# Attention queries stored per head over all 128 partitions, with the other head's rows zero

## The chip, the core and the metric

The kernel runs on one core of a Trainium2 chip. The metric is the device time of one execution in microseconds (us). Besides TensorE (PE, with its weight loads listed apart as PEld), the core has VectorE (DVE), ScalarE (ACT), GpSimd (POOL) and SyncE (SP), each with its own instruction queue.

## The reference, cut to what matters

One decoder layer over 512 tokens of 2048 channels: an RMS norm, one wide input projection, four token mixers (a gated linear recurrence, pooling, a short convolution, an attention), four gates, an output projection, and an MLP. The change is in the attention alone: 8 heads of 64 channels, queries and keys normalised per head, swept in 4 blocks of 128 queries.

```python
q = rms_norm(q.reshape(b, s, 8, 64), q_g)
k = rms_norm(k.reshape(b, s, 8, 64), k_g)
logits = einsum('bqhd,bkhd->bhqk', qi, k) * 64 ** -0.5
logits = logits + (cqi[..., :, None] - cum[..., None, :])
p = softmax(where(key_pos <= q_pos, logits, -inf))
out = einsum('bhqk,bkhd->bqhd', p, v)
```

## The kernel before, in words

Activations lie transposed: channels on the 128 partitions, the 512 tokens along a row. Two neighbouring heads therefore share one tile: the even head lies on partitions 0 to 63, the odd head on 64 to 127. There are four such pairs.

Every large product runs in fp32 accuracy as three products (`mm3`, line 182): each operand is split into a high part rounded to fp32r and a low part, the rest (`split`, line 213: ACT writes the high part, line 218, or line 221 with a per-partition scale; DVE writes the low part, line 219, or line 222 with the scale). The first operand of `mm3` is the stationary one (it is loaded as weights), the second streams through.

Weights come in chunks of 1024 columns by DMA on SP's queue, are split by ACT (line 150) and DVE (line 151), and are held in three buffers, so that two chunks are ready while one is used (`chunk`, line 155).

For each pair `i`, `pair` (line 487) projects queries and keys and hands them to `qk_norm` (line 350), which computes the per-head norm and at its end, line 363, calls `split` into tiles of the tag "m" (16 buffers of 128x512). Four tiles of "m" hold the values throughout. Then `attend` (line 427) does for each of 4 query blocks `t` and both heads `b` what `probabilities` (line 439) says: one `mm3` of a 128-token query block (stationary) against the keys up to it (streaming 256, 256, 384 or 512 columns) into a bank `pl`, the forget bias (DVE, line 446), the causal mask (POOL, line 450), the softmax (DVE and ACT, lines 455 to 458). It takes the head's half of the tiles, `r = slice(64 * b, 64 * b + 64)`, so these products use 64 of the 128 rows of the array. Next come the transposes of the probabilities (`pt`, line 179), their copy (`pT`, ACT, line 475) and the product with the values (`po`, line 480), whose output takes 64 of the 128 columns of the array.

The order on PE is that of the program text. The attention steps are generators that are resumed from within the projections: `poll` (line 203), called after each `mm3` of a projection, resumes a step when a counter of estimated PE time has passed its due time. The counter uses the number of columns of a product, not its rows. So each attention step stands alone between projection products (`pgb`, `pq`, `pk`, `pb` and so on, 128 rows by 512 columns). The order on ACT and DVE up to line 1121 is chosen at build time by the framework's scheduler; from there on it is that of the text.

After the attention (it ends near 530 us) follow the gates, the output projection and the MLP in a Strassen-like form with products of 128x256, from about 640 us to the end.

Of the kernel before, what the change touches and what calls it, by code (L numbers as in the profile page):

```python
# [15 lines left out]
P = 128  # L16
# [82 lines left out]
def body(nc, tc, ctx, dram):  # L99
# [3 lines left out]
    V, A, G, T = nc.vector, nc.scalar, nc.gpsimd, nc.tensor  # L103

    def const(name, shape, dt=F32):
        return pool.tile(shape, dt, name=name, tag=f"c_{name}", bufs=1)
# [18 lines left out]
    def t512(tag, name, dt=F32, rows=P):  # L125
        return stage[tag].tile([rows, S], dt, name=name, tag=tag, bufs=BUFS[tag])

    def bank(name, tag="mm"):
        return psum.tile([P, 512], F32, name=name, tag=tag, bufs=4)

    def f(x):
        return x.bitcast(F32)
# [39 lines left out]
    def mm(out, w, x, start, stop, more=False):  # L172
        T.matmul(out, w, x, start=start, stop=stop, skip_group_check=more)  # L173
        n = x.shape[-1]
        clock[0] += (max(n, 2 * P) if x.dtype == F32R else 4 * max(n, P)) / 2400

    def tr(out, x):
        n = x.shape[0]
        T.transpose(out, x, ident[:n, :n])
        clock[0] += P / 1200  # L180

    def mm3(out, w, x, first=True, last=True, more=False):

        n = x[0].shape[-1]
        mm(out[:, :n], w[0], x[0], first, False, more)
        mm(out[:, :n], w[0], x[1], False, False, more)
        mm(out[:, :n], w[1], x[0], False, last, more)
# [25 lines left out]
    def split(src, tag, name, scale=None):  # L213

        hi = t512(tag, f"{name}h", F32R)
        lo = t512(tag, f"{name}l", F32R)
        if scale is None:
            A.copy(hi, src)
            V.tensor_tensor(out=lo, in0=src, in1=f(hi), op=ALU.subtract)
        else:  # L220
            A.mul(hi, src, scale)
            V.scalar_tensor_tensor(out=lo, in0=src, scalar=scale, in1=f(hi), op0=ALU.mult, op1=ALU.subtract)
        return hi, lo
# [15 lines left out]
    def pc(name, i=0, rows=P):  # L239
        c = _COLS[name][0] + i  # L240
        return par[:rows, c : c + 1]
# [7 lines left out]
    for k in range(KT):  # L249
        h, r = divmod(k, 8)  # L250
# [37 lines left out]
    def inv_sqrt(y, ms, v, s):  # L288

        A.activation(s, ms, AF.Sqrt)  # L290
        recip(y, s)
        V.tensor_tensor(out=v, in0=ms, in1=y, op=ALU.mult)
        V.tensor_tensor(out=v, in0=v, in1=y, op=ALU.mult)
        V.tensor_scalar(v, v, -0.5, 1.5, ALU.mult, ALU.add)
        V.tensor_tensor(out=y, in0=y, in1=v, op=ALU.mult)
# [45 lines left out]
    def proj(c, name, given=None, tag="y"):  # L341
# [2 lines left out]
        V.tensor_tensor(out=o, in0=ps, in1=n1[1], op=ALU.mult)  # L344
        return o

    qg8 = const("qg8", [P, 1])
    V.tensor_scalar(qg8, pc("qg"), 0.125, None, ALU.mult)

    def qk_norm(src, g, name):  # L350
        sq = t512("y", f"{name}sq")
        A.activation(sq, src, AF.Square)
        hi, lo = split(sq, "y", f"{name}q")
        yield 10
        ms = bank(f"{name}ms", "aux")
        mm(ms, eblk, hi, True, False)
        mm(ms, eblk, lo, False, True)
        v, s = t512("y", f"{name}v"), t512("y", f"{name}s")
        V.tensor_scalar(v, ms, EPS, None, ALU.add)
        inv_sqrt(sq, v, v, s)  # L360
        V.scalar_tensor_tensor(out=src, in0=src, scalar=g, in1=sq, op0=ALU.mult, op1=ALU.mult)
        yield 5
        qk[name] = split(src, "m", f"{name}n")

    def log1p_exp_neg_abs(z, mk, name):

# [28 lines left out]
    qk = {}  # L395
# [31 lines left out]
    def attend(i):  # L427
        qn, kn = qk[f"q{i}"], qk[f"k{i}"]
        y = t512("k", f"yd{i}")
        ys[3].append(y)  # L430
        ncb = []
        for b in range(2):
            h = 2 * i + b
            n = t512("g", f"ncb{h}")
            nc.sync.dma_start(n, ncd[h : h + 1].to_broadcast([P, S]))
            ncb.append(n)
        yield 4

        def probabilities(t, b):
            h = 2 * i + b  # L440
            r = slice(64 * b, 64 * b + 64)
            span = (t + 1) * P
            pl = bank(f"pl{h}{t}", "aux")
            mm3(pl, [p[r, t * P : span] for p in qn], [p[r, : max(span, 2 * P)] for p in kn])
            l = t512("y", f"l{h}{t}")
            V.scalar_tensor_tensor(
                out=l[:, :span], in0=ncb[b][:, :span], scalar=cumT[:, t * 8 + h : t * 8 + h + 1],
                in1=pl[:, :span], op0=ALU.add, op1=ALU.add,
            )
            G.affine_select(  # L450
                out=l[:, t * P : span], in_=l[:, t * P : span], compare_op=ALU.is_ge, fill=NEG,
                base=0, pattern=[[-1, P]], channel_multiplier=1,
            )
            st = pool.tile([P, 4], F32, name=f"st{h}{t}", tag="st", bufs=6)
            V.tensor_reduce(st[:, 0:1], l[:, :span], axis=AX.X, op=ALU.max, negate=True)
            A.activation(l[:, :span], l[:, :span], AF.Exp, bias=st[:, 0:1], accum_out=st[:, 1:2])
            V.reciprocal(st[:, 2:3], st[:, 1:2])
            V.tensor_scalar(l[:, :span], l[:, :span], st[:, 2:3], None, ALU.mult)
            return l

        steps = [(t, b) for t in range(TT) for b in range(2)]
        ahead = [probabilities(*steps[0])]
        yield 4
        ahead.append(probabilities(*steps[1]))
        for n, (t, b) in enumerate(steps):
            h = 2 * i + b
            yield 4
            l = ahead.pop(0)
            if n + 2 < len(steps):
                ahead.append(probabilities(*steps[n + 2]))  # L470
            pt = bank(f"pt{h}{t}", "aux")
            for k in range(t + 1):
                tr(pt[:, k * P : (k + 1) * P], l[:, k * P : (k + 1) * P])
            pT = t512("y", f"pT{h}{t}")
            A.copy(pT[:, : (t + 1) * P], pt[:, : (t + 1) * P])
            yield 4
            if b == 0:
                po = bank(f"po{i}{t}", "aux")
            for k in range(t + 1):
                mm(  # L480
                    po[64 * b : 64 * b + 64, :P], val[k][:, h * 64 : (h + 1) * 64],
                    pT[:, k * P : (k + 1) * P], k == 0, k == t,
                )
            if b == 1:
                A.copy(y[:, t * P : (t + 1) * P], po[:, :P])

    def pair(i):
        q = proj(XQ + i * P, f"q{i}")
        chain(qk_norm(q, qg8, f"q{i}"))
        k = proj(XK + i * P, f"k{i}")  # L490

        def steps():
            yield from qk_norm(k, pc("kg"), f"k{i}")
            yield 12
            yield from attend(i)

        chain(steps())
# [7 lines left out]
    for t in range(TT):  # L505
        V.tensor_scalar(zt[:, t * 8 : (t + 1) * 8], vb[t][:, nv:VW], n1[0][:, t : t + 1], None, ALU.mult)
        A.mul(val[t][:, W - nv :], vb[t][:, :nv], n1[0][:, t : t + 1])
    chain(forget(zt))
    chain(qk_norm(first[0], qg8, "q0"))


# [308 lines left out]
    def result(name, where, tag, cols):  # L820

        for t in list(later):
            if t[3] < era[0]:
                pop(t)
        era[0] += 1
        return wide(name, where, tag, 2, cols)
# [107 lines left out]
    def wide(name, where, tag, bufs, cols=7 * H):  # L934
        return where[1].tile([P, cols], F32, name=name, tag=tag, bufs=bufs)

    def half_wide(name, where):
        return wide(name, where, "u", 1, S)
# [122 lines left out]
    for k in range(4):  # L1061
# [24 lines left out]
        if k == 3:  # L1086
            yk = y3

            p, ip = t512("p", "p"), t512("p", "ip")
# [8 lines left out]
        else:  # L1098
            yk, y3 = y2, [split(y, "s", f"y3{q}") for q, y in enumerate(ys[3])]
            for j in (6, 7, 0, 1, 2, 3, 4, 5):  # L1100
                x = wide(f"x_{j}", lz[0], "z", 2, 1024)
                t = wide(f"xs{j}", st1, "st1", 1)
# [10 lines left out]
        for j in range(8):  # L1113
            for e, ps in rows(f"branch{k}", 0, j, yk, f"pb{k}"):
                n = 2 * j + e
                t = t512("g", f"b{k}{n}")
# [105 lines left out]
    for e in range(2):  # L1222
        hi, lo = (t512("q", f"mg{q}{7 + 8 * e}", F32R) for q in "hl")
        src = merged[0][:, e * S : (e + 1) * S]
# [178 lines left out]
    for n, phase in enumerate(down_pairs, 2):  # L1403
        r, u = result(f"y{n}", dpool, "r", 1024), half_wide(f"ud{n}", dpool)
# [97 lines left out]
```

## Time and profile before

| | us |
|---|---|
| median of 3 runs | 2746.12 (2743.14 to 2746.85) |
| the profiled execution's own time | 2745.49 |
| span of its trace | 2743.7 |
| PE busy | 2711.5 (99% of the span) |
| PEld busy | 2544.5 (93%) |
| DVE busy | 2137.7 (78%) |
| ACT busy | 1223.0 (45%) |
| POOL busy | 156.5 (6%) |

The profile is of one execution of the 2745.49 us. A busy PE is not a PE at its peak: a product is recorded from its start to a modelled end, which overlaps the next one. What a product costs in a stream is the distance from its start to the next start; the timeline shows it. Mean granted clock of PE: 0.997 of full speed.

### The profile page before, as it was taken

Reading aid. Unit: us, or ns where it says so; the run is one execution under the profiler, and the core shown is the slowest. Engines: PE = TensorE matmul, PEld = TensorE weight load, DVE = VectorE, ACT = ScalarE, POOL = GpSimd, SP = SyncE. Lnnn points to the kernel's source line nnn. Section 1 sums busy time; section 2 is a strip of 40 time slices with the busy share of each in tenths; the row PEclk is TensorE's granted clock in tenths of the full one; section 3 lists DMA queues with packets and bytes.
Section 4 is the critical chain, followed back from the end, with each engine's and each line's share of the span. In section 5 each row is a group of like instructions: output and inputs, shape, how many; then the busy total and the mean of one; then the engine's idle time right before and its main releaser. Section 6 shows DMA issues by size and latency. Waiting matters only on the chain. (4 is left out here: it accounts for less than half of the span.)

```text
span 2743.7 us, 48190 instructions
## 1 busy us (share of the span) xinstructions
PE 2711.5 (99%) x19952; PEld 2544.5 (93%) x19952; DVE 2137.7 (78%) x2641; ACT 1223.0 (45%) x1506; POOL 156.5 (6%) x283
## 2 busy tenths in 40 slices
PE   8999999999999999999999999999998999999999
PEld 7787777789999999998888999999998999999999
DVE  6865664386888888887549988888887788888887
ACT  5443344454444444443324444444444444444443
POOL 0000000000000000003010000000000000000000
PEclk9999999999999999999999999999999999999999
DMA  5222223474444444447453544444446656666575
GB/s 198 86 93 85 81 81 125 163 231 159 145 154 147 152 133 155 143 142 256 144 176 123 173 164 145 163 148 161 149 141 228 183 177 182 182 174 190 169 217 145
DMA packets 143900, 429.48 MB, mean 157 GB/s; under 512 B 16696, under 2 KB 30904, under 8 KB 143680
## 3 DMA queue, kind: packets, MB, share of 16 engines
q1 hardware_dynamic: 101536, 279.19, 29.9%
q0 software_dynamic: 32496, 129.65, 16.2%
q10 hardware_dynamic: 9648, 17.57, 1.7%
q8 instruction: 156, 2.56, 0.4%
q14 instruction: 64, 0.52, 0.1%
HBM read 350.04 MB, written 79.97 MB: 157 GB/s over the span
## 5 line engine op out<-in xcount | busy, mean ns | idle before, releaser
L731 ACT CAST uhd<-wqd 128x1024 fp32r<-128x1024 f32 (+2 forms) x128 | 130.8, 1024 | 230.3 <-PE pdd L173 86.8
L731 ACT CAST uhg<-wqg 128x1024 fp32r<-128x1024 f32 (+1 forms) x136 | 135.5, 999 | 184.8 <-PE pgd L173 94.3
L731 ACT CAST uhu<-wqu 128x1024 fp32r<-128x1024 f32 (+1 forms) x144 | 136.2, 952 | 160.1 <-PE pud L173 85.2
L741 DVE TENSOR_TENSOR uld<-wqd,uhd 128x1024 fp32r<-128x1024 f32 (+2 forms) x128 | 151.8, 1187 | 69.6 <-ACT uhd L731 69.6
L151 DVE TENSOR_TENSOR wl<-wr,wh 128x1024 fp32r<-128x1024 f32 (+2 forms) x100 | 117.4, 1175 | 91.1 <-ACT wh L150 90.8
L741 DVE TENSOR_TENSOR ulg<-wqg,uhg 128x1024 fp32r<-128x1024 f32 (+1 forms) x136 | 157.1, 1157 | 31.7 <-ACT uhg L731 31.7
L150 ACT CAST wh<-wr 128x1024 fp32r<-128x1024 f32 (+2 forms) x100 | 101.3, 1014 | 159.2 <-PE pb L173 33.1
L731 ACT CAST uhg<-zg 128x1024 fp32r<-128x1024 f32 (+1 forms) x102 | 102.0, 1000 | 150.8 <-DVE ulg L741 101.6
L741 DVE TENSOR_TENSOR ulu<-wqu,uhu 128x1024 fp32r<-128x1024 f32 (+1 forms) x144 | 157.6, 1099 | 7.7 <-ACT uhu L731 7.6
L731 ACT CAST uhu<-zu 128x1024 fp32r<-128x1024 f32 (+1 forms) x108 | 103.1, 955 | 124.6 <-DVE ulu L741 72.0
L731 ACT CAST uhd<-zd 128x1024 fp32r<-128x1024 f32 x90 | 94.5, 1050 | 105.7 <-PE pdb L173 55.7
L173 PE MATMUL pda<-shd,uld 128*128 128x256 f32 x480 | 134.5, 280 | 0.0
L173 PE MATMUL pda<-sld,uhd 128*128 128x256 f32 x480 | 134.5, 280 | 0.0
L173 PE MATMUL pdd<-shd,uld 128*128 128x256 f32 x480 | 134.5, 280 | 0.0
L173 PE MATMUL pda<-shd,uhd 128*128 128x256 f32 x480 | 134.5, 280 | 0.0
L173 PE MATMUL pdb<-shd,uld 128*128 128x256 f32 x480 | 134.5, 280 | 0.0
L173 PE MATMUL pdb<-shd,uhd 128*128 128x256 f32 x480 | 134.5, 280 | 0.0
L173 PE MATMUL pdd<-shd,uhd 128*128 128x256 f32 x480 | 134.4, 280 | 0.0
L173 PE MATMUL pdd<-sld,uhd 128*128 128x256 f32 x480 | 134.4, 280 | 0.0
L173 PE MATMUL pdb<-sld,uhd 128*128 128x256 f32 x480 | 134.4, 280 | 0.0
L173 PE MATMUL pgd<-shg,ulg 128*128 128x256 f32 x480 | 134.2, 280 | 0.0
L173 PE MATMUL pgb<-shg,ulg 128*128 128x256 f32 x480 | 134.2, 280 | 0.0
(1473 smaller groups left out, 10436.3 us busy)
## 6 DMA issues: line engine op xcount, KB each, us to landing
wqg<-in_w SPq DMA_DIRECT2D x120, 512.0 KB, 3.5
wqu<-in_w SPq DMA_DIRECT2D x112, 512.0 KB, 3.5
wr<-in_w SPq DMA_DIRECT2D x84, 512.0 KB, 3.5
std<-zd POOLq DMA_DIRECT2D x39, 896.0 KB, 4.9
zd<-h POOLq DMA_DIRECT2D x32, 896.0 KB, 4.8
bk<-b ACTq DMA_DIRECT2D x64, 256.0 KB, 2.4
b<-bk POOLq DMA_DIRECT2D x32, 512.0 KB, 4.7
wo<-in_w SPq DMA_DIRECT2D x32, 512.0 KB, 3.7
```

Source lines behind the costliest of these rows:

```text
L150: A.copy(hi, raw)
L151: V.tensor_tensor(out=lo, in0=raw, in1=f(hi), op=ALU.subtract)
L173: T.matmul(out, w, x, start=start, stop=stop, skip_group_check=more)
L731: A.copy(self.hi[:, sl], self.phase.source(i))
L741: V.tensor_tensor(out=lo, in0=self.phase.source(i), in1=f(hi), op=ALU.subtract)
```

## The change

A tile `head` of 128x2 is set up: column `b` is one on the partitions of head `b` of a pair and zero on the others. `qk_norm` splits the queries twice, once with each column as the per-partition scale, so that there are four query tiles for a pair in place of two: one high and one low part for each head, with zeros on the other head's partitions. The keys are split as before. The product with the keys then runs over all 128 partitions; the zero rows take the other head out of the sum.

```diff
     qg8 = const("qg8", [P, 1])
+    head = const("head", [P, 2])
+    V.memset(head, 0.0)
+    for b in range(2):
+        V.memset(head[64 * b : 64 * b + 64, b : b + 1], 1.0)
     V.tensor_scalar(qg8, pc("qg"), 0.125, None, ALU.mult)
...
         yield 5
-        qk[name] = split(src, "m", f"{name}n")
+        if name[0] == "q":
+            qk[name] = [split(src, "m", f"{name}n{b}", head[:, b : b + 1]) for b in range(2)]
+        else:
+            qk[name] = split(src, "m", f"{name}n")
...
         def probabilities(t, b):
             h = 2 * i + b
-            r = slice(64 * b, 64 * b + 64)
             span = (t + 1) * P
             pl = bank(f"pl{h}{t}", "aux")
-            mm3(pl, [p[r, t * P : span] for p in qn], [p[r, : max(span, 2 * P)] for p in kn])
+            mm3(pl, [p[:, t * P : span] for p in qn[b]], [p[:, : max(span, 2 * P)] for p in kn])
```

## Rows read from the trace of the kernel before

**Rows 1.** Stages: busy us of PE, PEld, DVE, ACT, POOL (instructions), PEclk, DMA share, GB/s

```profile
440.00:520.00 80.00, 77.60 (x340) 58.56 (x340) 26.04 (x39) 32.67 (x61) 2.68 (x6) 0.96 0.41 145
700.00:2743.00 2043.00, 2023.11 (x16492) 1988.69 (x16490) 1682.70 (x1979) 908.76 (x1041) 131.05 (x226) 1.00 0.52 166
```

**Rows 2.** Waits of PE, 170 to 520 us, all of them: us, times, longest

```profile
PE pb L173 <- DVE y10l L219: 1.3, 1, 1.3
PE po L173 <- ACT pT L475: 1.2, 2, 1.0
PE pb L173 <- ACT y10h L218: 1.1, 1, 1.1
```

**Rows 3.** PE timeline, key product with no transpose behind it: start us, us, operation, tiles, shapes

```profile
288.44 0.39 PE L173 MATMUL pgb<-x14l,wh 128*128 128x512 f32 x1
288.67 0.40 PE L173 MATMUL pgb<-x14h,wl 128*128 128x512 f32 x1
289.00 0.39 PE L173 MATMUL pl<-k1nh,q1nh 64*128 64x256 f32 x1
289.22 0.28 PE L173 MATMUL pl<-k1nl,q1nh 64*128 64x256 f32 x1
289.34 0.28 PE L173 MATMUL pl<-k1nh,q1nl 64*128 64x256 f32 x1
289.55 0.51 PE L173 MATMUL pgb<-x15h,wh 128*128 128x512 f32 x1
289.89 0.39 PE L173 MATMUL pgb<-x15l,wh 128*128 128x512 f32 x1
```

**Rows 4.** PE timeline in the gates: 128 rows by 256 columns in a stream

```profile
1000.01 0.28 PE L173 MATMUL pgd<-shg,ulg 128*128 128x256 f32 x1
1000.13 0.28 PE L173 MATMUL pgd<-shg,uhg 128*128 128x256 f32 x1
```

**Rows 5.** PE timeline, three transposes right behind a key product

```profile
232.43 0.55 PE L179 MATMUL pt<-ident,l 128*128 128x128 f32 x3
...
233.05 0.39 PE L173 MATMUL pq<-x11l,wh 128*128 128x512 f32 x1
```

**Rows 6.** PE timeline, four transposes between projection products

```profile
255.42 0.60 PE L179 MATMUL pt<-ident,l 128*128 128x128 f32 x4
...
256.09 0.39 PE L173 MATMUL pgc<-x6l,wh 128*128 128x512 f32 x1
```

**Rows 7.** PE timeline, value products right ahead of a key product

```profile
386.93 1.09 PE L173 MATMUL po<-pT,val 128*64 128x128 f32 x8
387.94 0.46 PE L173 MATMUL pl<-k2nh,q2nh 64*128 64x384 f32 x1
```

**Rows 8.** Tile pl: count, duration ns min/median/max, first and last start, forms

```profile
L173 PE MATMUL pl<-k1nh,q1nh x8: 381/412/497, 289.0 to 357.7; 64*128 64x256 f32 x4, 64*128 64x384 f32 x2, 64*128 64x512 f32 x2
L173 PE MATMUL pl<-k2nh,q2nh x8: 381/413/497, 354.8 to 423.1; 64*128 64x256 f32 x4, 64*128 64x384 f32 x2, 64*128 64x512 f32 x2
```

**Rows 9.** Lines of the splits and of a small memset: ns min/median/max, first and last start

```profile
L218 ACT CAST q1nh<-q x1: 617/617/617, 262.1 to 262.1; 128x512 fp32r<-128x512 f32 x1
L219 DVE TENSOR_TENSOR q1nl<-q,q1nh x1: 692/692/692, 262.7 to 262.7; 128x512 fp32r<-128x512 f32 x1
L221 ACT ACTIVATE x0h<-xr,gm x1: 721/721/721, 6.1 to 6.1; 128x512 fp32r<-128x512 f32 x1
L222 DVE SCALAR_TENSOR_TENSOR x0l<-xr,gm,x0h x1: 750/750/750, 6.8 to 6.8; 128x512 fp32r<-128x512 f32 x1
L280 DVE MEMSET eblkf<- x2: 112/112/112, 29.5 to 30.4; 64x64 f32 x2
```

**Rows 10.** PE timeline around the longest stall of the attention

```profile
487.80 0.55 PE L179 MATMUL pt<-ident,l 128*128 128x128 f32 x3
...
491.91 0.63 PE L173 MATMUL pb<-y10h,wl 128*128 128x512 f32 x1
...
496.60 0.40 PE L173 MATMUL pb<-y10l,wh 128*128 128x512 f32 x1
```

## The prediction

> **What bounds the kernel.** I read the busy times by stage first, then PE's waits, then PE's timeline around the attention. From 700 us on PE is busy 2023.11 of 2043.00 us, while DVE has 1682.70 and ACT 908.76 [rows 1]: PE sets the pace there, and what is gained ahead of it is kept. In the attention the list of PE's waits is short: from 170 to 520 us it holds three lines, 3.6 us together, none of them for a weight, a query or a key [rows 2]. So within the attention too the time is what PE's own stream takes, and the question is what a start costs in it. The reader should take distances between starts, since the recorded durations overlap.
>
> The stream around a key product is uneven. A 512-column product between two others takes 0.23 us (288.44 to 288.67). The last one ahead of the key products takes 0.33, the first key product 0.22, the second 0.12, the third 0.21, the first projection product behind them 0.34 (289.55 to 289.89) [rows 3]. The second, which has its own kind on both sides, gives the plain price of 256 columns: 0.12 us. Hence four places with about 0.10 us too much: 0.10 ahead of the change from 128 rows to 64, 0.10 behind it, 0.09 ahead of the change back, 0.11 behind it. They come where the shape of the used array changes, and not where merely the output tile or the weights change.
>
> **The change part by part.**
>
> *The key products.* There are 32 groups of three (4 pairs, 4 blocks, 2 heads; 8 for each pair [rows 8]). With 128 rows on both sides the four extras should go. What a 128-row product of 256 columns costs in a stream is on record: 0.12 us (1000.01 to 1000.13) [rows 4], the same as the 64-row one. So the wider product itself costs nothing more, and only the extras count.
>
> - Entering: 0.10 + 0.10 = 0.20 us. In 4 of the 32 groups the value products, which use 64 columns of the array, stand right ahead (8 of them from 386.93, and the key product follows at 387.94 [rows 7]); there a change of shape stays, and I count no gain. 28 x 0.20 = 5.6 us.
> - Leaving, ahead of the change: 32 x 0.09 = 2.9 us.
> - Leaving, behind it: 8 groups are followed by a projection product, 8 x 0.11 = 0.9 us. The other 24 are followed by transposes, which hide part of it. Three transposes and one projection product behind a key product take 0.62 us (232.43 to 233.05) [rows 5]; four transposes and one product with nothing narrow near them take 0.67 (255.42 to 256.09) [rows 6]. Counting one transpose at 0.10 us, three would take 0.57, so 0.05 goes; over the 24 I take 0.04, 1.0 us. Its bounds are 0 (the transposes hide all) and 0.11 (as without them, 2.6 us).
>
> The sum is 5.6 + 2.9 + 0.9 + 1.0 = 10.4 us, with bounds of 9.4 and 12.0.
>
> *The splits.* The queries of a pair are split twice with a scale. The scaled forms take 0.72 us on ACT and 0.75 on DVE, the plain ones 0.62 and 0.69 [rows 9]. For a pair that adds 2 x 0.72 - 0.62 = 0.82 us on ACT and 2 x 0.75 - 0.69 = 0.81 on DVE; for four pairs 3.3 and 3.2 us. On the path to PE I cost them at nothing. What hides them: the low part of pair 1 is started at 262.7 us [rows 9] and first used at 289.0 [rows 8], 26 us later; and work queued behind the splits on ACT and DVE (the weight splits, the softmax, the copies `pT`) does not hold PE in this stretch except for 1.2 us on `pT` [rows 2]. If all that cover were gone, it would cost 6.5 us, which makes the time about 2742.
>
> *The memsets.* Three small ones on DVE, each nearest to the 64x64 one of 0.11 us [rows 9], 0.3 us long before the queries are split; nothing on PE, at most that 0.3.
>
> *The buffers.* A pair now holds 6 tiles of "m" in place of 4. Pairs 1 and 2 overlap: the first product of pair 2 starts at 354.8, the last of pair 1 at 357.7 [rows 8]. Values 4 + 6 + 6 = 16, just the buffers there are. The pair before has been read to its end long before new queries come, so I cost this at nothing. With one buffer fewer it would not be slow: pair 2's products stand ahead of pair 1's last on PE, so the wait would never end.
>
> *What is late next.* The largest stall of this stretch stays: three transposes at 487.80, then projection products that wait for `y10h` and `y10l` [rows 2, 10]. From 487.80 to 496.60 there are three transposes and 13 products; at 0.10 and 0.23 us they would take 3.3, and they take 8.8. Of the 5.5 us lost, 2.4 are the two waits [rows 2]; behind the idle time the granted clock fell to the lower of its two levels, 1.2 in place of 2.4 GHz (the 11 products from 491.91 to 496.60 stand 0.43 apart; the mean clock from 440 to 520 is 0.96 [rows 1]). DVE reaches `y10l` only behind the softmax of the key product just ahead of it, so the stall moves with PE's stream and gives nothing back of what was gained earlier.
>
> *Against a rule.* In the stream a 64-row product costs what a 128-row one does, 0.12 us [rows 3, 4]. The Trainium skill, TensorEngine Tiling (Array Packing), sections Theoretical Speedup and When to Use Tiling, speaks against this change: with a contraction of at most 64 it says to split the array by rows, for up to twice the speed. By that rule the change gives up a gain; by the rows no such gain is being had, since the three products that follow each other belong to one head and use the same half. What it would cost is the second rival.
>
> **Sum.** The profiled execution took 2745.49 us; less 10.4 that is 2735.1. The median of the runs shown is 0.6 higher, so for a median I say 2735.7.
>
> **Rivals.**
>
> 1. *The extras are not the row count's* (0.08): if they belonged to something else that starts a key product, its weights or its bank, they stay, and the added splits stay hidden: 2746. Against it: the second key product has other weights than the first and shows no extra [rows 3], and four transposes start a new bank with new weights and show none either (0.67 us is 4 x 0.10 + 0.23 and 0.04 more) [rows 6].
>
> 2. *The halves of the array did overlap* (0.03, slower): if a 64-row product now costs half of what it would over all rows, each of 96 products doubles. With 0.12 us for 256 columns, 0.23 for 512 and 0.175 between, that is 24 x (0.12 + 0.12 + 0.175 + 0.23) = 15.5 us, less 10.4 gained: 2751. It decides as soon as the doubling is over two thirds of that. Rows 4 speak against it.
>
> 3. *The added splits turn into stalls* (0.07 for one, 0.03 for three): the scheduler orders ACT and DVE anew around more work, at the queries of pairs 1, 2 and 3, and a weight split or a `pT` copy comes too late; PE idles and its clock falls. The price of one such stall is the 5.5 us of [rows 10]. One makes 2741; two cancel the gain, which is where this decides; three make 2752, slower. For it: the one long stall that there is comes from just such a place in DVE's queue. Against it: the weights are two chunks ahead, and PE waits for none today [rows 2].
>
> 4. *The stall at 488 us goes* (0.05), because another order puts `y10l` ahead of the softmax: 2730.
>
> **How the numbers follow.** The forecast, 2735.7, has 0.74. A measurement of this kernel can tell about 0.2%, 5.5 us, from no change. Faster by more than that: the forecast, rival 4 and a part of the one-stall case, 0.81. Within it: rival 1 and the rest of one stall, 0.13. Slower: rival 2 and three stalls, 0.06. The range 2731 to 2743 holds the forecast with the bounds of its terms (2734 to 2737), the one stall (2741) and the splits uncovered (2742); left out are 2730, 2746, 2751 and 2752, 0.19 together.
>
> **What would show it.** In the timeline of the changed kernel: the product ahead of a key product at 0.23 us, the first key product at 0.12, the third at 0.12, the next projection product at 0.23; entries behind value products as before. Key products listed as 128 rows. In the waits, no new line for weights or queries. The stall near 480 us (8 us earlier than before) of the same size. Wrong if the extras are still there at 128 rows, if the key products stand more than 0.12 us apart at 256 columns, or if new waits of PE of several us appear between 260 and 440 us.

## The result, and the profile of the changed kernel

The changed kernel takes 2731.06 us (median of 5 runs, 2729.84 to 2733.16), the kernel before 2745.40 (5 runs beside them). The ratio is 0.995, its 95% interval 0.9939 to 0.996: faster by 14.3 us, where 10.4 were forecast. The profiled execution took 2731.06 us, its span is 2729.3, against 2743.7 before. The busy times of the changed kernel's engines, from the top of its page:

```profile
PE 2697.3 (99%) x19952; PEld 2543.4 (93%) x19952; DVE 2140.0 (78%) x2648; ACT 1226.1 (45%) x1510; POOL 156.7 (6%) x283
```

PE has lost 14.2 us of busy time with the same number of instructions. DVE and ACT have gained 2.3 and 3.1 us.

The PE timeline of the changed kernel at the places of [rows 5], [rows 3] and [rows 7], start us and us first:

```profile
229.73 0.49 PE L179 MATMUL pt<-ident,l 128*128 128x128 f32 x3
...
230.29 0.39 PE L173 MATMUL pq<-x11l,wh 128*128 128x512 f32 x1
...
285.46 0.39 PE L173 MATMUL pgb<-x14h,wl 128*128 128x512 f32 x1
285.69 0.28 PE L173 MATMUL pl<-k1nh,q1n0h 128*128 128x256 f32 x1
285.81 0.28 PE L173 MATMUL pl<-k1nl,q1n0h 128*128 128x256 f32 x1
285.93 0.28 PE L173 MATMUL pl<-k1nh,q1n0l 128*128 128x256 f32 x1
286.05 0.39 PE L173 MATMUL pgb<-x15h,wh 128*128 128x512 f32 x1
286.28 0.39 PE L173 MATMUL pgb<-x15l,wh 128*128 128x512 f32 x1
...
380.80 0.44 PE L173 MATMUL pl<-k2nh,q2n0h 128*128 128x384 f32 x1
381.08 0.34 PE L173 MATMUL pl<-k2nl,q2n0h 128*128 128x384 f32 x1
381.26 0.34 PE L173 MATMUL pl<-k2nh,q2n0l 128*128 128x384 f32 x1
```

From 285.46 the distances are now 0.23, 0.12, 0.12, 0.12, 0.23: no extra is left at any of the four places. Three transposes and a projection product behind a key product take 0.56 us (229.73 to 230.29) in place of 0.62 [rows 5]. Behind value products [rows 7] the first key product still takes 0.10 more than the next (0.28 and 0.18).

The weight loads show the same place from another side. PEld at the first key product of [rows 3], in the kernel before and in the changed one (a square bracket gives the idle time ahead of a line and what ended it; "issue" means that the profile shows no wait):

```profile
288.99 0.18 PEld L173 LDWEIGHTS pl<-k1nh,q1nh 64*128 64x128 f32 x1 [0.37 <-issue]
285.46 0.19 PEld L173 LDWEIGHTS pl<-k1nh,q1n0h 128*128 128x128 f32 x1
```

Before, the weights of that product are loaded only as it starts (289.00). In the changed kernel they are loaded from the start of the product ahead of it (285.46), 0.23 us before their own product starts (285.69). The late load stands at every change of shape in the kernel before: from 174 to 520 us there are 120, and at each the load starts at most 0.003 us before its product; where the shape stays, the median is 0.23.

The splits of a pair's queries for one head, from the views of their tiles (they answer to [rows 9]); the three memsets of `head` take 0.06 us each, at 1 us:

```profile
L221 ACT ACTIVATE q1n0h<-q,head x1: 722/722/722, 258.9 to 258.9; 128x512 fp32r<-128x512 f32 x1
L222 DVE SCALAR_TENSOR_TENSOR q1n0l<-q,head,q1n0h x1: 750/750/750, 259.7 to 259.7; 128x512 fp32r<-128x512 f32 x1
```

All waits of PE from 160 to 510 us, in the form of [rows 2]:

```profile
PE po L173 <- ACT pT L482: 1.6, 2, 1.0
PE pb L173 <- ACT y10h L218: 1.4, 1, 1.4
PE pb L173 <- DVE y10l L219: 1.3, 1, 1.3
PE pt L179 <- DVE l L465: 0.4, 1, 0.4
```

One line is new, 0.4 us for a softmax; none is for a weight, a query or a key. The stall of [rows 10] is there, 10 us earlier:

```profile
477.71 0.49 PE L179 MATMUL pt<-ident,l 128*128 128x128 f32 x3
479.57 0.50 PE L173 MATMUL pb<-y10h,wh 128*128 128x512 f32 x1 [1.37 <-ACT y10h L218]
481.32 0.57 PE L173 MATMUL pb<-y10l,wh 128*128 128x512 f32 x1 [1.25 <-DVE y10l L219]
...
485.77 0.40 PE L173 MATMUL pb<-y10l,wh 128*128 128x512 f32 x1
```

It takes 8.06 us in place of 8.80. The mean clock of the stretch from 440 to 520 us is 0.98, where it was 0.96 [rows 1]; fewer products ran at the lower level.

**Where the 14.4 us of the span went.** Starts of the same products mark the stretches: the first key product, the first product of the last branch tile (`y33h`), the first `pdp` of the last stage, and the last product. PE timeline of the kernel before, then of the changed one:

```profile
175.30 0.38 PE L173 MATMUL pl<-k0nh,q0nh 64*128 64x256 f32 x1
591.38 0.39 PE L173 MATMUL pb<-y33h,wh 128*128 128x512 f32 x1
2092.09 0.41 PE L173 MATMUL pdp<-shd,uhd 128*128 128x256 f32 x1
2740.11 0.28 PE L173 MATMUL pdd<-shd,uld 128*128 128x256 f32 x1
```

```profile
174.33 0.28 PE L173 MATMUL pl<-k0nh,q0n0h 128*128 128x256 f32 x1
580.33 0.39 PE L173 MATMUL pb<-y33h,wh 128*128 128x512 f32 x1
2081.06 0.28 PE L173 MATMUL pdp<-shd,uhd 128*128 128x256 f32 x1
2725.71 0.28 PE L173 MATMUL pdd<-shd,uld 128*128 128x256 f32 x1
```

| stretch | before | after | gain |
|---|---|---|---|
| to the first key product | 175.30 | 174.33 | 0.97 |
| attention and branch products | 416.08 | 406.00 | 10.08 |
| end of the branch products, gates, output projection, MLP up | 1500.71 | 1500.73 | -0.02 |
| MLP down (last stage) | 648.02 | 644.65 | 3.37 |

The attention gives about what was forecast. The 0.97 us ahead of the first key product cannot be credited to the change: over the twelve kernels of the next section that product starts at 173.8 to 176.0 us, with no order that follows the edits. The last stage, which the change does not touch, gives 3.4 us more. There the gain grows evenly. The same two products, in the kernel before and in the changed one:

```profile
2222.86 0.28 PE L173 MATMUL pdd<-shd,uld 128*128 128x256 f32 x1
2665.89 0.28 PE L173 MATMUL pdb<-shd,uld 128*128 128x256 f32 x1
```

```profile
2211.22 0.28 PE L173 MATMUL pdd<-shd,uld 128*128 128x256 f32 x1
2651.83 0.28 PE L173 MATMUL pdb<-shd,uld 128*128 128x256 f32 x1
```

They stand 443.03 us apart before and 440.61 after: the stream of 128x256 products is 0.55% faster. Below, "last-stage distance" is the distance of these two products, and "attention" the second stretch of the table.

### The profile page after: what moved, and what is told of

Read it like the earlier page. It is cut to its first block, busy times and chain, and to the rows that moved or that the text cites. A ratio compares the mean times of both kernels' runs of the same rounds, so it can differ in the third digit from the quotient of the medians.

```text
span 2729.3 us, 48201 instructions
## 1 busy us (share of the span) xinstructions
PE 2697.3 (99%) x19952; PEld 2543.4 (93%) x19952; DVE 2140.0 (78%) x2648; ACT 1226.1 (45%) x1510; POOL 156.7 (6%) x283
## 5 line engine op out<-in xcount | busy, mean ns | idle before, releaser
L173 PE MATMUL pga<-shg,ulg 128*128 128x256 f32 x480 | 134.2, 280 | 0.0
L173 PE MATMUL pga<-shg,uhg 128*128 128x256 f32 x480 | 134.0, 279 | 0.0
L173 PE MATMUL pgb<-shg,uhg 128*128 128x256 f32 x480 | 134.0, 279 | 0.0
L173 PE MATMUL pgd<-shg,uhg 128*128 128x256 f32 x480 | 134.0, 279 | 0.0
```

## The experiments

The theory: a product on 64 rows between products on 128 costs PE its change of shape, there and back, and nothing else in the change matters to the time but, perhaps, where the tiles lie. The rivals: the work added or its order makes the time; a narrow product costs by itself; the halves of the array overlapped; the last stage differs from run to run.

| kernel | us, median | ratio to before, 95% | attention | last-stage distance |
|---|---|---|---|---|
| before | 2745.40 | | 416.08 | 443.03 |
| changed | 2731.06 | 0.995 (0.9939 to 0.996) | 406.00 | 440.61 |
| e1 head tile only | 2742.69 | 0.9992 (0.9984 to 1.0001) | 415.46 | 440.61 |
| e2 splits only | 2741.41 | 0.9989 (0.998 to 0.9998) | 415.59 | 440.61 |
| e3 full rows only | 2734.48 | 0.9961 (0.9949 to 0.9974) | 404.63 | 443.03 |
| e4 middle product narrow | 2743.95 | 0.9999 (0.999 to 1.0008) | 416.46 | 440.61 |
| e7 changed, no shift | 2734.66 | 0.9965 (0.9952 to 0.9977) | 405.87 | 443.03 |
| e8 before, shift by 64 | 2744.36 | 0.9997 (0.9988 to 1.0006) | 416.17 | 441.60 |
| e6 changed, values full | 2721.39 | 0.9914 (0.99 to 0.9927) | 395.57 | 440.61 |
| e9 halves in turn | 2741.63 | 0.9988 (0.9979 to 0.9996) | 410.74 | 443.03 |
| e10 the copy first | 2737.92 | 0.9974 (0.9964 to 0.9983) | 407.76 | 443.03 |
| e11 in turn, values full | 2720.43 | 0.9911 (0.9897 to 0.9924) | 395.34 | 440.61 |

The last two columns are worked out from the starts of products in the one traced execution of each kernel. The medians and ratios come from runs made beside the kernel before, whose own medians there lay between 2744.70 and 2745.40.

**e1, the head tile alone.** To the kernel before:

```diff
     qg8 = const("qg8", [P, 1])
+    head = const("head", [P, 2])
+    V.memset(head, 0.0)
+    for b in range(2):
+        V.memset(head[64 * b : 64 * b + 64, b : b + 1], 1.0)
```

> The kernel before with the tile of ones and zeros and its three memsets, which nothing reads. Theory (the gain comes from products that no longer change the shape of the array): no change, 2745.4 us within 2, and products of the last stage at the pace they have before. Rival (part of the 14.3 us, the 3 us that are gained after 2090 us, comes from where the tiles behind the new one lie): about 2742, with a shorter distance between the 128x256 products of the last stage.

By the runs alone this is open: the interval of the ratio holds 1. The trace decides, and for the rival: the attention is nearly unchanged (415.46; the 0.6 us lie in the stall of [rows 10]), and the last-stage distance is 440.61 (2220.29 to 2660.90), to the hundredth that of the changed kernel. An unused tile is enough to make the last stage faster.

**e2, the splits alone.** To the changed kernel:

```diff
-            mm3(pl, [p[:, t * P : span] for p in qn[b]], [p[:, : max(span, 2 * P)] for p in kn])
+            r = slice(64 * b, 64 * b + 64)
+            mm3(pl, [p[r, t * P : span] for p in qn[b]], [p[r, : max(span, 2 * P)] for p in kn])
```

> The changed kernel, with the key products on the 64 rows of their head again: the added splits alone. Theory: the added work is hidden, 2745.4 us within 2, and all extras around the key products are back (0.33, 0.22, 0.12, 0.21, 0.34). Rival (the added work costs PE time): up to 6.5 us more, 2752. Rival (the order that the scheduler makes of the added work gives the gain): about 2731 with the extras still there.

2741.41 us, 1.3 under e1, within its range of runs. The 2745.4 expected is missed by 4.0 us because that figure left out the place of the tiles, which moves here too (440.61); e1 is what e2 has to be compared with. The attention takes 415.59 us, 0.13 more than with the tile alone, and the extras are all back:

```profile
287.44 0.38 PE L173 MATMUL pl<-k1nh,q1n0h 64*128 64x256 f32 x1
287.65 0.28 PE L173 MATMUL pl<-k1nl,q1n0h 64*128 64x256 f32 x1
287.77 0.28 PE L173 MATMUL pl<-k1nh,q1n0l 64*128 64x256 f32 x1
287.98 0.50 PE L173 MATMUL pgb<-x15h,wh 128*128 128x512 f32 x1
```

With the product ahead (start 287.11) and the one behind (288.32) the distances are 0.33, 0.21, 0.12, 0.21 and 0.34. So the added splits cost PE nothing, and neither they nor their order give the gain. The only edit between e2 and the changed kernel is the rows of the key products.

**e3, full rows without the splits.** To the kernel before:

```diff
-            r = slice(64 * b, 64 * b + 64)
...
-            mm3(pl, [p[r, t * P : span] for p in qn], [p[r, : max(span, 2 * P)] for p in kn])
+            mm3(pl, [p[:, t * P : span] for p in qn], [p[:, : max(span, 2 * P)] for p in kn])
```

> The kernel before, with queries split once as there, and the key products over all 128 rows: it leaves out the masking of the other head, so that each product sums over both heads. Theory: the whole gain without the added work, 2731 to 2735 us, the same as the changed kernel within 2. Rival (the added splits cost something even in the changed kernel): below the changed kernel by up to 6.5 us, 2725.

2734.48 us: the attention gains 11.45 us, and the last stage nothing (443.03). That is 3.4 us above the changed kernel and not the same within 2, since without the tile nothing moves; the kernel to compare it with is e7 below (2734.66). The 1.4 us by which its attention is ahead of the changed kernel's is not the splits: the two run level until 482 us and part in the stall there, where the changed kernel's clock is at the lower level for some products and this one's is not (mean granted clock from 478 to 486 us 0.79 and 1.00).

**e4, one narrow product of three.** To the changed kernel:

```diff
-            mm3(pl, [p[:, t * P : span] for p in qn[b]], [p[:, : max(span, 2 * P)] for p in kn])
+            r = slice(64 * b, 64 * b + 64)
+            qh, ql = (p[:, t * P : span] for p in qn[b])
+            kh, kl = (p[:, : max(span, 2 * P)] for p in kn)
+            n = max(span, 2 * P)
+            mm(pl[:, :n], qh, kh, True, False)
+            mm(pl[:, :n], qh[r], kl[r], False, False)
+            mm(pl[:, :n], ql, kh, False, True)
```

> The changed kernel, with the middle one of each three key products (low part of the keys) on the 64 rows of its head, the first and third on all 128. Theory (a change of shape costs, not a narrow product): two changes in each group as before, 32 x 0.4 = 12.8 us come back, 2744 within 2. Rival (each narrow product costs its share): a third of the gain is lost, 2731 + 4.8 = 2736.

2743.95 us: 12.9 us are lost again, where a third would be 4.8 at most. That it comes so near the 12.8 expected is partly luck: in the traces the attention loses 10.5 (416.46 and 406.00), and another 3.5 lie where the edit changes nothing (1.7 ahead of the first key product, 1.8 between the attention and the last stage). Even 10.5 is more than twice a third of the gain. The PE timeline shows where:

```profile
289.62 0.39 PE L173 MATMUL pgb<-x14h,wl 128*128 128x512 f32 x1
289.85 0.28 PE L173 MATMUL pl<-k1nh,q1n0h 128*128 128x256 f32 x1
290.06 0.38 PE L173 MATMUL pl<-k1nl,q1n0h 64*128 64x256 f32 x1
290.37 0.38 PE L173 MATMUL pl<-k1nh,q1n0l 128*128 128x256 f32 x1
290.59 0.40 PE L173 MATMUL pgb<-x15h,wh 128*128 128x512 f32 x1
```

The three take 0.21, 0.31 and 0.22 us in place of 0.12 each, 0.38 together for one narrow product, and the projection products on either side are back at 0.23. What costs is each change of shape: about 0.10 us ahead of it and 0.10 behind it, whichever way it goes. The Trainium skill, TensorEngine Tiling (Array Packing), Key Properties, says that changing the tiling mode drains TensorE, and gives no size. The trace agrees: the extras stand at the changes of shape alone.

**e7 and e8, where the later tiles lie.** The allocation gives the head tile 32 bytes of each partition, so that tiles placed behind it move by 32 bytes. In e7 (to the changed kernel) the two columns are put where no tile of the last stage moves; in e8 (to the kernel before) an unused tile takes 64 bytes.

```diff
-    qg8 = const("qg8", [P, 1])
-    head = const("head", [P, 2])
+    qg8 = const("qg8", [P, 3])
+    qg8, head = qg8[:, :1], qg8[:, 1:]
```

```diff
     qg8 = const("qg8", [P, 1])
+    head = const("head", [P, 16])
+    V.memset(head, 0.0)
```

> The changed kernel, with the two columns of the head tile put into the 32 bytes that the one-column tile beside it takes anyway, so that no later tile lies elsewhere than before. Theory (the 3 us gained after 2090 us come from the shift of the later tiles by 32 bytes): 2734 us, and the 128x256 products of the last stage 0.1179 us apart as before, not 0.1172. Rival (they come from something else in the change, or from run to run): 2731 and 0.1172.

> The kernel before, with an unused tile of 64 bytes in each partition at the place of the head tile: a shift of the later tiles by 64 bytes instead of 32. If it is the place within 64 bytes that matters, the products of the last stage stand 0.1179 us apart as before (2745 us); if any shift does it, 0.1172 (2742).

e7 takes 2734.66 us (2733.59 to 2736.69, no overlap with the changed kernel's runs), with the attention of the changed kernel (405.87) and the last stage of the one before. Its two products:

```profile
2212.03 0.28 PE L173 MATMUL pdd<-shd,uld 128*128 128x256 f32 x1
2655.06 0.28 PE L173 MATMUL pdb<-shd,uld 128*128 128x256 f32 x1
```

443.03 us apart again. So the 3 us hang on the place of the tiles behind the head tile. e8 fits neither of its two cases: 441.60, a gain of 1.4 us over this distance where 32 bytes give 2.4. It is not simply the place within 64 bytes, and not any shift alike. Six kernels with a shift of 32 bytes show 440.61, five without a shift 443.03, so run to run is ruled out. By the addresses in the built programs, the operands of these products hardly move: all the weight tiles (`uhd`, `uld`) and 35 of the 39 pairs of streamed tiles (`shd`, `sld`) lie at the same place in the kernel before and in the changed one. So what matters is mostly not where the products' own operands lie. Which of the moved tiles it is, and by what path it slows the products, was not tried and stays open.

**e6, the value products made full as well.** To the changed kernel (only the head's half of each bank is used):

```diff
-            if b == 0:
-                po = bank(f"po{i}{t}", "aux")
+            r = slice(64 * b, 64 * b + 64)
+            po = bank(f"po{h}{t}", "aux")
             for k in range(t + 1):
                 mm(
-                    po[64 * b : 64 * b + 64, :P], val[k][:, h * 64 : (h + 1) * 64],
+                    po[:, :P], val[k][:, i * P : (i + 1) * P],
                     pT[:, k * P : (k + 1) * P], k == 0, k == t,
                 )
-            if b == 1:
-                A.copy(y[:, t * P : (t + 1) * P], po[:, :P])
+            A.copy(y[r, t * P : (t + 1) * P], po[r, :P])
```

> The changed kernel, with the value products also over the whole array: the stationary operand is the pair's 128 value columns instead of the head's 64, each head has a bank of its own, and only the head's half of the output is copied (one small copy more on ACT for each query block and pair). Theory: the extras around the 32 groups of value products go as well. In the trace of the changed kernel the projection product ahead of them takes 0.33 us, six of them 0.80 in place of about 0.64, the product behind 0.34: 0.10 + 0.16 + 0.11 = 0.37 for a group, 32 x 0.37 = 11.8 us, so about 2719 us, within 3. Rival (the extras belong to 64 rows only): no gain, 2731.

2721.39 us: another 9.7 us, 10.4 of the attention. The same group of value products, first in the changed kernel, then in e6:

```profile
487.39 0.40 PE L173 MATMUL pb<-y12h,wl 128*128 128x512 f32 x1
487.72 0.87 PE L173 MATMUL po<-pT,val 128*64 128x128 f32 x6
488.52 0.50 PE L173 MATMUL pb<-y13h,wh 128*128 128x512 f32 x1
488.86 0.40 PE L173 MATMUL pb<-y13l,wh 128*128 128x512 f32 x1
```

```profile
490.22 0.39 PE L173 MATMUL pb<-y10h,wl 128*128 128x512 f32 x1
490.45 0.83 PE L173 MATMUL po<-pT,val 128*128 128x128 f32 x6
491.04 0.48 PE L173 MATMUL pb<-y11h,wh 128*128 128x512 f32 x1
491.35 0.39 PE L173 MATMUL pb<-y11l,wh 128*128 128x512 f32 x1
```

1.47 us become 1.13. The product behind keeps most of its extra (0.31 in place of 0.34), which is why it is a little less than the 11.8 expected. That rest is not a change of shape: behind three transposes of full shape the product of the changed kernel takes 0.32 as well (229.97 to 230.29). Within a group the value products stand 0.11 us apart with 64 columns and with 128. So a half-width output costs like a half-height input, at its changes of shape and not by itself.

**e9, e10 and e11, do the halves overlap?** In e9 (to the kernel before) the products of both heads of a query block are issued in turn, each head on its half of the rows; the softmax of both follows. In e10 these stand behind the transposes and the copy `pT` of the step, in e11 the value products of e6 and an unused tile that takes 32 bytes come on top. The core of e9:

```diff
+            for x, (c, d) in enumerate(((0, 0), (0, 1), (1, 0))):
+                for b in range(2):
+                    r = slice(64 * b, 64 * b + 64)
+                    mm(pls[b][:, :n], qn[c][r, t * P : span], kn[d][r, :n], x == 0, x == 2)
```

> The kernel before, with the key products of both heads of a query block issued together, in turn: head on rows 0 to 63, head on rows 64 to 127, three times. Half of the changes of shape go: 16 x (0.33 to 0.41) = 5.3 to 6.6 us. Theory (products on different halves do not overlap): 2739 to 2740. Rival (they do overlap, up to twice the speed): another 7.7 us, 2732, and the six products of 256 columns no more than 0.06 us apart.

> The kernel with the heads' products in turn, with the products of the next query block moved behind the transposes and the copy pT of the current one, so that this copy stands ahead of their softmax in ACT's queue. Theory (the halves overlap, and what they gained was given back by one wait of 7.5 us for pT and the lower clock behind it): that wait goes, 2741.6 - 7.5 - 1.2, about 2733, within 3. Rival (overlap gains little and the wait only moves): 2739 or more.

> The same, with the value products over all 128 columns as in the run before (e6) and an unused tile of 8 bytes at the place of the head tile, which shifts the later tiles by 32 bytes; queries are not split per head. Theory (the three gains add up): 2733 - 11 - 3 = 2719, within 3, at or a little below the kernel with full key and value products (2721.4). Rival (a new wait takes one of them): 2724 or more.

They do overlap. The PE timeline of e9 at the place of [rows 3]; each line stands for two products, one on each half:

```profile
284.63 0.39 PE L173 MATMUL pl<-k1nh,q1nh 64*128 64x256 f32 x2
284.86 0.28 PE L173 MATMUL pl<-k1nl,q1nh 64*128 64x256 f32 x2
284.98 0.28 PE L173 MATMUL pl<-k1nh,q1nl 64*128 64x256 f32 x2
285.18 0.51 PE L173 MATMUL pgb<-x15h,wh 128*128 128x512 f32 x1
```

Six products take 0.55 us (284.63 to 285.18), as three did before (289.00 to 289.55 [rows 3]). The Trainium skill, TensorEngine Tiling (Array Packing), Key Properties, says that different tiles of the array can execute matmuls in parallel; the trace agrees, since the two products of a line start within 0.004 us of each other. Yet e9 is faster by only 3.1 us, 2741.63, where neither the theory (2739 to 2740) nor the rival (2732) had it. Its waits of PE from 160 to 640 us begin with a new one:

```profile
PE po L173 <- ACT pT L481: 9.3, 3, 7.5
```

The copy `pT` stands behind a softmax on ACT, and the first step of that softmax (the bias on DVE) starts only at 392.24, behind the norm of the next pair's queries in DVE's queue, although its key products had all started by 382.8. That costs 7.5 us of PE up to 395.90, and the clock falls behind it (mean granted clock 0.71 from 396 to 402 us). With the order of e10 the line shrinks to 3.6 us, and the time by 3.7: 2737.92, which misses the 2733 expected and lies between theory and rival. Its attention gains 8.3 us over the kernel before, where the expectation of e9 had 13 to 14 for a full overlap, so part of the overlap is still given back. e11 is at 2720.43, 1.0 us from e6, within the ranges of both: 2719 within 3 was expected. With full value products, filling the array by zeros or by a second head comes to the same (attention 395.57 and 395.34), about 10 us faster than the changed kernel. With the value products as they were it does not: with nothing moved in either, the heads in turn (e10) are 3.3 us slower than zeros (e7, 2734.66).

## Why the prediction was right, and where it fell short

- **The four extras and their cause.** Right, in mechanism and not only in number. The extras are gone where all products use 128 rows, they come back with the rows (e2) and with one narrow product of three (e4), and they go without the splits (e3).
- **The sum in the attention, 10.4 us.** Right, and nearly so in each term. Both kernels issue the same products in the same order, so the gain can be read distance by distance. At the 32 groups the extras gave 10.4 us: 5.6 entering (forecast 5.6), 2.7 leaving ahead of the change (2.9), 0.9 behind it with a projection product (0.9), 1.3 with transposes (1.0; 0.055 for a group in place of 0.04). Two small misses cancel there. The groups behind value products kept their entry extra as forecast. That the whole stretch shows 10.08 has some luck in it: the stall gave 0.74 more, because less of it ran at the lower clock, and a new wait for a softmax and a longer one for `pT` took about 0.9, and the forecast had neither.
- **The added splits, nothing.** Right: 0.13 us between e1 and e2. Their sizes, 0.72 and 0.75 us, were as taken. The new wait of 0.4 us is not theirs: e3, which lacks them, has it too.
- **The buffers, nothing.** No wait on them appears.
- **The stall, of the same size.** Nearly: 8.06 in place of 8.80 us, and 10 us earlier in place of 8. Its two waits are there; the number of products at the lower clock is not fixed by them.
- **Behind the attention, kept.** Right for the 1500 us up to the last stage (-0.02 us).
- **The memsets and the head tile, nothing.** Here the working failed. The three memsets cost nothing (0.06 us each, at 1 us). But the tile that they fill was taken to have no cost and no gain at all; it moves the tiles placed behind it by 32 bytes, and the last stage is about 3 us shorter for it (3.4 with the tile alone in e1; 2.7 between e7 and the changed kernel). With the 1.0 us ahead of the first key product, which the change does not explain, that is why 14.3 us came and not 10.4.
- **The range.** That 2731.06 falls inside 2731 to 2743 is luck: by 0.06 us, and two of the five runs lie below 2731. The range began there only to leave out the 2730 of the fourth rival, and no term of it stood for the place of tiles. The same change with nothing moved in the last stage (e7) takes 2734.66, inside the 2734 to 2737 that the terms gave.
- **The rivals.** The extras come with the change of the row count (e2, e4), the splits make no stall, the stall at 488 us does not go. That the halves overlapped in the kernel before is wrong, since three products of one head follow each other; but they do overlap as soon as the halves alternate (e9). A stall like that of the third rival did appear in e9, where the order of the key products was changed.

## What to carry to other kernels

A narrow product among full ones costs PE its change of shape, here 0.3 to 0.4 us there and back, so a few narrow products scattered through a full stream are better made full with zeros or with output that is thrown away, if the operand can be prepared beside PE. Narrow products on different halves overlap when they are issued in turn, but then the softmax behind them needs its place in the other queues looked at; with that place only half mended (e10) zeros were still faster. An added tile, however small, moves others: where a stage that a change does not touch gets faster or slower, put the tile where nothing moves before crediting the change.

## What the runs showed of the hardware that was not expected

- A shift of tiles by 32 bytes of each partition changes the pace of a stream of 128x256 fp32r products in the last stage, though few of their own operands move: 443.03 us without it (five kernels), 440.61 with it (six), 441.60 with 64 bytes (one). The stretch from the attention to the last stage shows no such order: 1500.71 us before, 1500.73 in the changed kernel, 1500.2 to 1502.5 over all twelve.
- Where the shape of the used array changes, the weights of the next product are loaded only as it starts (at most 0.003 us ahead of it, at all 120 changes of the kernel before), and not during the product ahead of it as in a stream of one shape (median 0.23 us ahead).
- Six products on alternating halves of the rows take the time of three on one half (0.55 us).
- After a stall with the same two waits (2.4 to 2.6 us together), the mean granted clock differed: 0.62 in the kernel before (488 to 497 us, 11 products at the lower level), 0.79 in the changed kernel and 1.00 in e3 (478 to 486 us).
